# Fused two-matrix product with tanh: six plain row tiles in place of eight, the first weight slices by a second queue, a new order of all engines, and the last products' finish shared otherwise

## The chip, the cores and the metric

One core of a Trainium2 chip. The time is the device time of one execution in microseconds (us), the median of several. A span is the same execution as the hardware profiler sees it; on this kernel it is 1.7 to 2.2 us shorter than the device time. Engines are called TensorE (PE in the profile, its weight loads PEld), VectorE (DVE), ScalarE (ACT), GpSimd (POOL) and SyncE (SP, which here only issues transfers).

## The reference

```python
x: (16, 512, 1024) f32, w1, w2: (1024, 768) f32
y1 = np.matmul(x, w1)
y2 = np.matmul(x, w2)
return (np.tanh(y1) * y2).astype(np.float32)
```

There are 8192 rows, that is 64 row tiles of 128.

## The kernel before

The first `HEAD` row tiles are multiplied the plain way in bf16, while the weights are still arriving. All others go in pairs through a recursive scheme (Strassen's): seven products of half size (p1 to p7) in place of eight, in f16, on sums and differences of blocks of x (s1 to s4) and of w (t1 to t4). A "unit" is one pair with one of the two weights. Each half-size product is 4 matmuls of 384 columns, so a pair costs 2 x 7 x 4 = 56.

```python
HEAD = 8
WARM = 14                                         # matmuls on constants at the very start
PAIRS = (MT - HEAD) // 2
LOADS = ("x0 a0 x1 a1 x2 a2 x3 a3 a4 a5 a6 a7 b0 b1 b2 b3 b4 b5 b6 b7").split()   # x tiles; slices of w1 (a), w2 (b)
FILL = {"m00G0": 16, "m10G0": 4, "m20F0": 4}      # matmuls on constants, ahead of these
ORDER = {"pe": """T00 T01 m00G0 m00F0 T10 T11 ...""", "act": """...""", "dve": """...""", "dma": """..."""}   # [cut]
```

`ORDER` fixes each engine's queue for the head and the first ten units. In its names Tij is a transpose of an x tile on TensorE, mijFk and mijGk are plain matmuls of 512 and 256 columns (tile i, weight j, slice k), Lp, ax, rx, cx and Tx are a later x tile's load, sum of absolute values, scale, cast and transpose by DMA, and b11a ... t4b are weight blocks. From unit 10 on, times in slots of 0.65 us set the order. I call the seam between the two "the join".

```python
def load_w(t, k):
    pin(nc.sync.dma_start(w_f[t][:, k, :], wr[t][:, k, :]))

def product(i, t, n, bank, start, stop, cols=slice(0, Q)):
    a, b = PRODUCTS[n]
    for k in range(KH):                                     # four matmuls
        pin(nc.tensor.matmul(bank[:, cols], st[i, a][:, k, :], wt[t][b][:, k, cols], ...))

# a unit, cut to what the text needs
"p1":   pe               "seed": act, copies p1's bank, needs p1
"p6":   pe, needs seed   "c12", "c22": dve, sums of banks
"p4":   pe, needs c22    "f..": the outputs (tanh on act, multiply on dve)

# the last two units: GpSimd takes over two multiplies
if u == UNITS - 1:
    for h, c, due in ((0, "c12", 4.1), (1, "c22", 4.8)):
        ops[f"f{h}1"] = ("pool", 0.85, due, [c], final_pool, (u, c, h))
        ops[f"store{h}1"] = ("dma", 0.5, due + 0.1, [f"f{h}1"], store, (i, h, high, nc.scalar))

# later pairs
at(slot(z - 25), scale_x, i)
for h in range(2):
    at(slot(z - 24 + 4 * h), cast_x, i, h, "dve")
    at(slot(z - 24 + 4 * h), transpose_x, i, h)
```

## Time and profile before

| | before |
|---|---|
| time, median of the first 3 runs | 319.98 us (319.44 to 320.25) |
| profiled execution | 320.89 us, span 319.0 |
| first transposes of x0, of x1 on TensorE | 4.22 us, 8.13 us |
| first recursive product | 51.22 us |
| stop at the join | 101.60 to 102.34 and 103.64 to 104.26: 1.36 us |
| start of the last product to the end of the span | 5.12 us |

The chain of waits follows the run back from its last instruction, so it shows what sets the time; a list of waits shows only what an engine waited for; the timeline of TensorE shows also what it did in place of waiting. The prediction shows these lines.

### The profile page before, as it was taken

Reading aid. Unit: us, or ns where it says so; the run is one execution under the profiler, and the core shown is the slowest. Engines: PE = TensorE matmul, PEld = TensorE weight load, DVE = VectorE, ACT = ScalarE, POOL = GpSimd, SP = SyncE. Lnnn points to the kernel's source line nnn. Section 1 sums busy time; section 2 is a strip of 40 time slices with the busy share of each in tenths; the row PEclk is TensorE's granted clock in tenths of the full one; section 3 lists DMA queues with packets and bytes.
Section 4 is the critical chain, followed back from the end, with each engine's and each line's share of the span. In section 5 each row is a group of like instructions: output and inputs, shape, how many; then the busy total and the mean of one; then the engine's idle time right before and its main releaser. Section 6 shows DMA issues by size and latency. Waiting matters only on the chain.

```text
span 319.0 us, 5509 instructions
## 1 busy us (share of the span) xinstructions
PE 310.9 (97%) x1924; PEld 188.1 (59%) x1930; DVE 241.1 (76%) x559; ACT 227.6 (71%) x442; POOL 5.1 (2%) x10
## 2 busy tenths in 40 slices
PE   8999999999999999999999999999999999999994
PEld 5665665666555565555556565555555655555652
DVE  2557899686887897777778877777798777778742
ACT  1767896787767677787777778787777787776551
POOL 0000000000000000000000000000000000000004
PEclk9999999999999999999999999999999999999999
DMA  7999189969989999899999898998998999986222
GB/s 246 408 400 408 54 229 285 255 205 214 343 247 269 281 294 283 243 278 275 251 241 257 262 235 275 283 265 248 255 249 262 230 286 274 247 234 166 99 101 100
DMA packets 80187, 80.05 MB, mean 251 GB/s; under 512 B 61472, under 2 KB 61984, under 8 KB 80160
## 3 DMA queue, kind: packets, MB, share of 16 engines
q1 hardware_dynamic: 79872, 79.31, 87.7%
q8 instruction: 15, 0.25, 0.3%
q10 hardware_dynamic: 288, 0.39, 0.3%
q14 instruction: 12, 0.10, 0.1%
HBM read 39.85 MB, written 25.17 MB: 204 GB/s over the span
## 4 chain that ended last, share of the span: by engine, by line
PE 89%; DMA 8%; ACT 1%; DVE 1%; issue 0%; SPq 0%
PE bank L405 80%; DMA wf<-in_w_dram 6%; PE bank L271 5%; PE bank L274 3%; DMA x_f<-in_x_dram 2%; PE bank L243 1%; ACT junk L344 0%; DVE wb L258 0%; DVE o L441 0%; ACT th L435 0%; SPq L254 0%; SPq L217 0%; ACT bank L418 0%; DVE wp0r L354 0%; DVE w_inv L352 0%
## 5 line engine op out<-in xcount | busy, mean ns | idle before, releaser
L405 PE MATMUL bank<-t,s 128*128 128x384 f16 x672 | 127.6, 326 | 0.6 <-ACT u L422 0.6
L405 PEld LDWEIGHTS <-s 128*128 128x128 f16 x896 | 87.5, 98 | 59.4 <-issue 1.5
L405 PEld LDWEIGHTS <-xT 128*128 128x128 f16 x672 | 65.6, 98 | 45.3 <-issue 1.1
L405 PE MATMUL bank<-b,xT 128*128 128x384 f16 x448 | 90.6, 326 | 0.5 <-ACT bank L418 0.5
L427 DVE TENSOR_TENSOR c<-bank,u 128x384 f32<-128x384 f32 x56 | 31.0, 554 | 46.1 <-PE bank L405 45.6
L344 ACT ACTIVATE junk<-x_f 128x1024 bf16<-128x1024 f32 x56 | 58.7, 1049 | 1.7 <-DMA x_f<-in_x_dram 1.6
L435 ACT ACTIVATE th<-c,out_r 128x384 f32<-128x384 f32 x56 | 33.9, 609 | 23.2 <-DVE c L427 23.2
L405 PE MATMUL bank<-b,s 128*128 128x384 f16 x224 | 45.4, 326 | 0.0
L405 PE MATMUL bank<-t,xT 128*128 128x384 f16 x224 | 45.3, 325 | 0.0
L422 ACT ACTIVATE u<-bank 128x384 f32<-128x384 f32 x56 | 27.3, 488 | 20.1 <-PE bank L405 19.5
L364 DVE TENSOR_SCALAR x_h<-x_f,pr 128x1024 f16<-128x1024 f32 x54 | 40.1, 747 | 0.1
L435 ACT ACTIVATE th<-bank,out_r 128x384 f32<-128x384 f32 x56 | 32.2, 575 | 6.0 <-PE bank L405 6.0
L441 DVE SCALAR_TENSOR_TENSOR o<-bank,out_r,th 128x384 f32<-128x384 f32 x56 | 34.2, 611 | 2.9 <-PE bank L405 2.8
L418 ACT ACTIVATE bank<-bank 128x384 f32<-128x384 f32 x56 | 27.0, 483 | 9.9 <-DVE o L441 8.7
L427 DVE TENSOR_TENSOR c<-bank,s 128x384 f32<-128x384 f32 x56 | 31.0, 554 | 3.8 <-ACT th L435 1.3
L422 ACT ACTIVATE s<-bank 128x384 f32<-128x384 f32 x56 | 26.9, 483 | 8.3 <-PE bank L405 6.0
L441 DVE SCALAR_TENSOR_TENSOR o<-c,out_r,th 128x384 f32<-128x384 f32 x54 | 32.5, 607 | 0.1
L271 PE MATMUL bank<-wb,xTb 128*128 128x512 bf16 x122 | 31.2, 379 | 0.5 <-DVE wb L258 0.2
L386 DVE TENSOR_TENSOR s<-xT 128x512 f16<-128x512 f16 x56 | 23.0, 416 | 0.0
L274 PE MATMUL bank<-wb,xTb 128*128 128x256 bf16 x128 | 19.2, 272 | 0.6 <-DVE wb L258 0.5
L271 PEld LDWEIGHTS <-xTb 128*128 128x128 bf16 x128 | 12.3, 98 | 11.6 <-issue 0.8
L274 PEld LDWEIGHTS <-xTb 128*128 128x128 bf16 x128 | 12.5, 99 | 5.1 <-issue 0.7
(51 smaller groups left out, 156.2 us busy)
## 6 DMA issues: line engine op xcount, KB each, us to landing
x_f<-in_x_dram SPq DMA_DIRECT2D x64, 512.0 KB, 6.2
out_dram<-o SPq DMA_DIRECT2D x62, 384.0 KB, 3.4
wf<-in_w_dram SPq DMA_DIRECT2D x16, 384.0 KB, 9.4
xT<-x_h SPq DMA_TRANSPOSE x56, 3.7
out_dram<-o ACTq DMA_DIRECT2D x2, 192.0 KB, 2.0
out_dram<-o SPq DMA_DIRECT2D x2, 192.0 KB, 2.4
```

The costliest lines, as they stand in the source:

```text
L243: pin(nc.tensor.transpose(b[:, k * P:(k + 1) * P], hb[mt][:, k * P:(k + 1) * P], ident_b))
L271: pin(nc.tensor.matmul(bank, hx[mt][:, k, :], w_b[t][k][:, :F], start=k == 0, stop=k == KO - 1))
L274: pin(nc.tensor.matmul(bank[:, at_:at_ + G], hx[mt][:, k, :], w_b[t][k][:, F:], start=k == 0 and mt % 2 == 0, stop=k == KO - 1, skip_group ...
L344: pin(nc.scalar.activation(junk[:, :K], xs[HEAD + 2 * i + h], ACT.Abs, scale=2.0 ** -12, accum_out=pair_sum[i][:, h:h + 1]))
L364: pin(nc.vector.tensor_scalar(xh, xs.pop(mt), pair_r[i][:, h:h + 1], None, ALU.mult))
L386: pin((nc.vector if eng == "dve" else nc.gpsimd).tensor_tensor(s, st[i, a], st[i, b], op))
L405: pin(nc.tensor.matmul(bank[:, cols], st[i, a][:, k, :], wt[t][b][:, k, cols], start=start and k == 0, stop=stop and k == KH - 1, skip_gro ...
L418: pin(nc.scalar.activation(ub[u]["b"][:, :Q], ub[u]["a"][:, :Q], ACT.Copy))
L422: pin(nc.scalar.activation(c, ub[u][bank][:, :Q], ACT.Copy))
L427: pin(nc.vector.tensor_tensor(c, ub[u][bank][:, :Q], ub[u][other], ALU.add))
L435: pin(nc.scalar.activation(th, v, ACT.Tanh, scale=rs[i][:, 0, h:h + 1]))
L441: pin(nc.vector.scalar_tensor_tensor(o[:, h, q * Q + cols.start:q * Q + cols.stop], v, rs[i][:, 1, h:h + 1], tanhs[i, h, q][:, cols], ALU. ...
```

## The change

The intent is to take work out of TensorE, which sets the time: two more tiles go through the recursive products. This leaves fewer plain matmuls to cover the time in which the weights' blocks are made, so the loads are started earlier (four slices of w1 by ScalarE's queue) and the order of all engines is made anew. At the end, half of GpSimd's second multiply goes to VectorE.

```diff
-    HEAD = 8
-    WARM = 14
+    HEAD = 6
+    WARM = 18
+    EARLY = ("La0", "La1", "La2", "La3")
-    FILL = {"m00G0": 16, "m10G0": 4, "m20F0": 4}
+    FILL = {"m00F0": 3, "m00F1": 6}
     ORDER = { ... all four lists new [cut] ... }
-                    at(start, fn, *args)
+                    at(0.0 if name in EARLY else start, fn, *args)
     def load_w(t, k):
-        pin(nc.sync.dma_start(w_f[t][:, k, :], wr[t][:, k, :]))
+        eng = nc.scalar if f"L{'ab'[t]}{k}" in EARLY else nc.sync
+        pin(eng.dma_start(w_f[t][:, k, :], wr[t][:, k, :]))
+        pool_cols = slice(0, Q), slice(Q // 2, Q)
-            for h, c, due in ((0, "c12", 4.1), (1, "c22", 4.8)):
-                ops[f"f{h}1"] = ("pool", 0.85, due, [c], final_pool, (u, c, h))
+            ops["f01"] = ("pool", 0.85, 4.1, ["c12"], final_pool, (u, "c12", 0, pool_cols[0]))
+            ops["f11b"] = ("pool", 0.5, 4.8, ["c22"], final_pool, (u, "c22", 1, pool_cols[1]))
+            ops["f11"] = ("dve", 0.4, 4.8, ["c22"], final, (u, "c22", 1, 1, slice(0, Q // 2)))
-        at(slot(z - 25), scale_x, i)
+        late = 1.1 * (i == FIRST + 1)
+        at(slot(z - 25 + late), scale_x, i)
         for h in range(2):
-            at(slot(z - 24 + 4 * h), cast_x, i, h, "dve")
-            at(slot(z - 24 + 4 * h), transpose_x, i, h)
+            at(slot(z - 24 + late + 4 * h), cast_x, i, h, "dve")
+            at(slot(z - 24 + late + 4 * h), transpose_x, i, h)
```

Cut: `ELSEWHERE`, which moves single operations to another engine, the planned durations of the first loads, and the stores that go with the new finish.

More of the change, by code (lines that the diff above doesn't have):

```diff
@@ L55 @@
                "t3": ("dve", 50), "t4": ("dve", 52)})
+    EARLY = ("La0", "La1", "La2", "La3")
     ELSEWHERE = {
-        "e01": "dve", "e11": "dve", "e31": "dve", "ca1": "act", "hx6": "act", "e71": "act", "cx30":
-        "act", "cx31": "act"
+        "e01": "dve", "e11": "dve", "e20": "act", "e21": "dve", "e31": "dve", "ca0": "act", "ca1": "act",
+        "cb4": "act", "b22a": "dve", "cx11": "act", "cx31": "act", "cx61": "act"
     }
-    FILL = {"m00G0": 16, "m10G0": 4, "m20F0": 4}
+    FILL = {"m00F0": 3, "m00F1": 6}
@@ L62 @@
     ORDER = {
         "pe": """
-            T00 T01 m00G0 m00F0 T10 T11 m10G0 m10F0 m00F1 m00G1 m10F1 T20 T21 m20F0 m20F1 m20G0 m20G1 m00G2
-            m10F2 m00F2 m20F2 T30 T31 m00G3 m10F3 m20F3 m00F3 m30F0 m30F1 m30F2 m30F3 m30G0 m30G1 m30G2 m20F4
-            m00G4 m10F4 m00F4 m00G5 m00F5 m10F5 m20F5 m30G3 m20G2 m20G3 m20G4 m10G1 m20G5 m10F6 m20G6 m00F6
-            m20F6 m10G2 m10G3 m10G4 m10G5 m10G6 m30G4 m30G5 m30G6 m00F7 m20F7 m20G7 m30G7 m10G7 m10F7 m30F4
-            m30F5 m30F6 m30F7 m21G0 m01F0 m11F0 m31G0 m11F1 m21G1 m31G1 m01F1 m01F2 m11F2 m31G2 m31G3 m01F3
@@ L69 @@
-            m31G4 m01F4 m11F3 suma m00G6 m00G7 m21G2 m21G3 m21G4 m11F4 m21F0 m21F1 m21F2 m21F3 m21F4 m21F5
-            m31G5 m01F5 m01F6 m11F5 m11F6 m31G6 m01F7 m11F7 m31G7 T4 m31F0 m31F1 m31F2 m31F3 m31F4 m31F5 m31F6
-            m31F7 m01G0 m11G0 m11G1 m11G2 m11G3 m01G1 m01G2 m01G3 m11G4 m11G5 m11G6 m01G4 m01G5 m11G7 m40F0
-            m40F1 m40F2 T5 m40F3 m40F4 m40F5 m40F6 m40F7 m01G6 m50F0 m01G7 m50F1 m50F2 m50F3 m50F4 m50F5 m50F6
-            m50F7 sumb m21G5 m21G6 m21G7 T6 m21F6 m21F7 m41F0 m41F1 m41F2 m41F3 m41F4 m41F5 m41F6 m41F7 T7
@@ L74 @@
-            m40G0 m50G0 m50G1 m40G1 m50G2 m50G3 m50G4 m50G5 m50G6 m40G2 m40G3 m40G4 m50G7 m40G5 m40G6 m40G7
-            m51F0 m51F1 m51F2 m51F3 m51F4 m51F5 m51F6 m51F7 m41G0 m41G1 m41G2 m41G3 m41G4 m41G5 m41G6 m41G7
-            m51G0 m51G1 m51G2 m51G3 m51G4 m51G5 m51G6 m51G7 m70F0 m70F1 m70F2 m70F3 m70F4 m70F5 m70F6 m70F7
-            m60F0 m60F1 m60F2 m60F3 m60F4 m60F5 m60F6 m60F7 m61F0 m61F1 m61F2 m61F3 m61F4 m61F5 m61F6 m61F7
-            p1.0 m60G0 m70G0 m60G1 m60G2 m60G3 m60G4 m70G1 p5.0 m70G2 m70G3 m70G4 m70G5 m70G6 m70G7 m60G5
@@ L79 @@
-            m60G6 m60G7 p2.0 p1.1 m71F0 m71F1 m71F2 m71F3 m71F4 m71F5 m71F6 m71F7 p6.0 p5.1 m61G0 m61G1 m61G2
-            m71G0 m71G1 m71G2 m71G3 m71G4 m71G5 p7.0 p2.1 m71G6 m61G3 m61G4 m61G5 m61G6 m61G7 p3.0 p4.0 p6.1
-            p1.2 p3.1 p7.1 m71G7 p5.2 p2.2 p4.1 p6.2 p1.3 p3.2 p7.2 p5.3 p2.3 p4.2 p6.3 p1.4 p3.3 p7.3 p5.4
-            p2.4 p6.4 p4.3 p1.5 p3.4 p7.4 p5.5 p2.5 p4.4 p6.5 p1.6 p3.5 p5.6 p7.5 p6.6 p2.6 p4.5 p1.7 p3.6
-            p6.7 p2.7 p5.7 p7.6 p7.7 p3.7 p4.6 p4.7 p1.8 p1.9 p5.8 p5.9 p3.8 p3.9 p6.8 p2.8 p7.8 p2.9 p1.10
@@ L84 @@
-            p4.8 p6.9 p7.9 p5.10 p2.10 p4.9
+            T00 T01 m00F0 m00G0 T10 T11 m00F1 m00G1 m10F0 T20 m10G0 m10G1 m10F1 T21 m20G0 m20F0 m20F1 m20G1
+            m10G2 m20G2 m00F2 m00G2 m20F2 m10F2 T30 T31 m10G3 m00G3 m20F3 m10F3 m20G3 m00F3 m10F4 m10G4 m20F4
+            m20G4 m00G4 m00F4 m30G0 m30G1 m30G2 m30G3 m20G5 m10G5 m10F5 m20F5 m20G6 m10G6 m10F6 m30G4 m30G5
+            m30G6 m20G7 m10G7 m30G7 m10F7 m00F5 m00F6 m00F7 suma m11F0 m20F6 m20F7 m01F0 m00G5 m00G6 m00G7
+            m11F1 m01F1 m30F0 m30F1 m30F2 m30F3 m30F4 m30F5 m30F6 m30F7 m21F0 m21F1 m11F2 m21F2 m01F2 m11F3
@@ new lines @@
+            m21F3 m01F3 m31F0 m31F1 m31F2 m31F3 m21G0 m21G1 m21G2 m21G3 m31G0 m31G1 m31G2 m31G3 m01F4 m31G4
+            m21G4 m11F4 m01G0 m01G1 m11G0 m11G1 m01G2 m01G3 m01G4 m31F4 T4 m11F5 m11F6 m01F5 m31F5 m01G5 m01G6
+            m31F6 m01F6 m31G5 m31G6 m01F7 m31F7 m11F7 m31G7 T5 m40F0 m40F1 m40F2 m40F3 m40F4 m40F5 m40F6 m01G7
+            m40F7 m21G5 m21G6 m50F0 m50F1 m50F2 m50F3 m50F4 m50F5 m50F6 m50F7 m21F4 m21F5 m21G7 m21F6 m21F7
+            m11G2 m11G3 m11G4 m11G5 m11G6 m11G7 m40G0 m50G0 m50G1 m50G2 m50G3 m50G4 m50G5 m50G6 m50G7 m40G1
@@ new lines @@
+            m40G2 m40G3 m40G4 m40G5 m40G6 m40G7 sumb m41F0 m41F1 m41F2 m41F3 m41F4 m41F5 m41F6 m41F7 m41G0
+            m41G1 m41G2 m41G3 m41G4 m41G5 m41G6 m51G0 m51G1 m51G2 m51G3 m51G4 m51G5 m51G6 m51G7 m41G7 m51F0
+            m51F1 m51F2 m51F3 m51F4 m51F5 m51F6 m51F7 p1.0 p1.1 p5.0 p6.0 p2.0 p3.0 p7.0 p5.1 p6.1 p4.0 p2.1
+            p7.1 p1.2 p3.1 p4.1 p1.3 p6.2 p2.2 p5.2 p6.3 p2.3 p5.3 p7.2 p7.3 p3.2 p4.2 p3.3 p4.3 p1.4 p1.5
+            p5.4 p5.5 p2.4 p6.4 p6.5 p2.5 p7.4 p7.5 p3.4 p3.5 p4.4 p4.5 p1.6 p1.7 p5.6 p6.6 p2.6 p6.7 p2.7
@@ L85 @@
+            p7.6 p3.6 p5.7 p7.7 p4.6 p3.7 p1.8 p4.7 p1.9 p2.8 p6.8 p5.8 p5.9 p7.8 p1.10 p3.8 p4.8 p3.9 p6.9
+            p2.9 p2.10 p7.9 p5.10 p4.9
         """,
         "act": """
-            ca1 absa1 absa0 e21 absa2 absa3 absa4 absa5 absa6 absa7 tanh2F tanh2G tanh1F absb2 absb4 tanh0G
-            absb7 tanh3F tanh0F absb0 absb6 b21a b22a hx6 tanh5F tanh4F ax00 ax01 e71 b11b tanh4G b22b ax11
-            b21b tanh7F tanh6F ax10 ax20 seed.0 ax30 tanh6G f00.0 ax21 u2.0 seed.1 ax31 s5.0 s5.1 f11.0 f01.0
@@ L90 @@
-            u2.1 f10.0 seed.2 ax41 s5.2 f00.2 u2.2 seed.3 cx30 f01.2 f11.2 s5.3 f10.2 u2.3 seed.4 cx31 s5.4
-            f00.4 u2.4 ax40 seed.5 f01.4 f11.4 s5.5 ax50 f10.4 u2.5 seed.6 s5.6 ax51 f00.6 seed.7 u2.6 u2.7
-            s5.7 ax61 ax60 f10.6 f11.6 f01.6 s5.8 s5.9 seed.8 u2.8 seed.9 f00.8 f11.8 f10.8 u2.9 f01.8 seed.10
-            s5.10 f00.10
+            ca0 absa0 ca1 absa1 e20 absa2 absa3 absa4 absa5 absa6 absa7 tanh2G absb0 tanh1F tanh0G tanh2F cb4
+            tanh0F absb2 absb6 tanh3F absb4 ax00 absb7 ax01 b21a tanh4F tanh5F ax10 ax11 tanh4G ax20 cx11 b11b
@@ L94 @@
+            b22b seed.0 seed.1 s5.0 u2.0 ax21 b21b u2.1 f00.0 s5.1 f10.0 ax31 seed.2 ax30 seed.3 f11.0 u2.2
+            u2.3 s5.2 s5.3 f00.2 f01.0 ax40 cx31 f10.2 seed.4 ax41 seed.5 s5.4 s5.5 u2.4 u2.5 f11.2 f00.4 ax51
+            f01.2 ax50 f10.4 seed.6 f11.4 seed.7 f01.4 u2.6 s5.6 ax61 u2.7 s5.7 f00.6 f11.6 f10.6 seed.8 ax60
+            f00.8 u2.8 f01.6 s5.8 cx61 s5.9 seed.9 f10.8 seed.10 u2.9 f01.8 f11.8 f00.10 s5.10
         """,
         "dve": """
-            e00 e01 ca0 e10 e11 e20 ca2 ca3 e30 ca4 ca5 ca6 e31 ca7 parta cb0 cb1 cb2 cb3 cb4 cb6 scalea cb5
@@ L97 @@
-            hx4 cb7 b11a t1a mul0F e41 hx5 mul1F e51 mul3F mul0G partb scaleb mul2G e61 hx7 mul2F mul4F rx0
-            sx0 cx00 cx01 t1b mul5F t2a mul4G t2b t4b t3b s3.0 s1.0 rx1 cx10 sx1 cx11 mul6F s2.0 s4.0 t3a t4a
-            mul7F rx2 sx2 cx20 cx21 c22.0 c12.0 s1.1 s2.1 s3.1 s4.1 c12.1 c22.1 mul6G f00.1 f11.1 f10.1 rx3
-            sx3 c12.2 c22.2 s3.2 s1.2 s2.2 f00.3 s4.2 f01.1 c12.3 f01.3 c22.3 f11.3 f10.3 c12.4 c22.4 s1.3
-            s3.3 s2.3 f00.5 rx4 cx40 sx4 cx41 c12.5 c22.5 f01.5 s4.3 f10.5 f11.5 rx5 cx50 sx5 f00.7 c12.6
@@ L102 @@
-            c22.6 c22.7 s1.4 s2.4 cx51 s4.4 s3.4 c12.7 rx6 cx60 f10.7 f11.7 f01.7 s1.5 s3.5 c22.8 cx61 c12.8
-            s2.5 s4.5 c12.9 f00.9 c22.9 f01.9 f10.9 f11.9
+            e00 e01 e10 e11 ca2 e21 ca3 ca4 e30 ca5 ca6 e31 ca7 parta cb0 cb1 scalea b11a cb2 cb3 t1a b22a hx4
+            cb6 cb5 t2a e41 cb7 hx5 mul0F mul3F mul1F e51 t3a rx0 cx00 cx01 mul2G mul2F mul0G partb t4a rx1
+            cx10 scaleb mul4F sx0 mul4G s1.0 s2.0 s4.0 s3.0 sx1 t1b t2b t3b c22.0 rx2 sx2 cx20 t4b s1.1 c22.1
@@ L104 @@
+            f00.1 s2.1 c12.0 f10.1 s3.1 cx21 c12.1 s4.1 f11.1 rx3 cx30 c22.2 c22.3 s3.2 s1.2 f00.3 f01.1 c12.2
+            c12.3 s2.2 f10.3 mul5F rx4 cx40 s4.2 cx41 s3.3 c22.4 f11.3 c22.5 f00.5 s1.3 c12.4 f01.3 s2.3 f10.5
+            rx5 f11.5 s4.3 cx50 c12.5 f01.5 c22.6 sx3 cx51 c22.7 f00.7 s1.4 s2.4 sx4 s3.4 c12.6 c12.7 rx6 cx60
+            s4.4 sx5 f01.7 c22.8 f10.7 f11.7 s1.5 s2.5 c12.8 s3.5 c12.9 f00.9 c22.9 s4.5 f11.9 f01.9 f10.9
         """,
         "dma": """
-            Lx0 La0 Lx1 La1 Lx2 La2 Lx3 La3 La4 La5 La6 La7 Lb0 Lb1 Lb2 Lb3 Lb4 Lb5 Lb6 Lx4 Lb7 Lx5 Lx6 Lx7
@@ L107 @@
-            Lp00 Lp01 Lp10 st2 Lp11 Tx00 Lp20 Tx01 Lp21 st4 Lp30 Lp31 Tx10 Lp40 Tx11 Lp41 Tx20 Lp50 Tx21 st7
-            st6 store1.1 Tx30 st3 store0.1 Tx31 Lp51 st5 st1 st0 Lp60 Tx40 Lp61 Tx41 store0.5 store1.5 Tx50
-            Lp70 Tx51 Lp71 Tx60 store0.7 store1.7 Tx61 store0.3 store0.9 store1.9 store1.3
+            Lx0 La0 Lx1 La1 Lx2 La2 Lx3 La3 La4 La5 La6 La7 Lb0 Lb1 Lb2 Lb3 Lb4 Lx4 Lb5 Lb6 Lx5 Lb7 Lp00 Lp01
+            Lp10 Lp11 Tx00 Lp20 Tx01 st3 Lp21 Tx10 Lp30 st4 Tx11 Lp31 st1 Tx20 Lp40 Lp41 Tx21 st2 Lp50 Tx30
@@ L110 @@
+            Lp51 Tx31 Lp60 st5 Tx40 Lp61 st0 Tx41 Lp70 store1.5 Tx50 store0.5 Lp71 Tx51 store0.1 store1.1 Tx60
+            store0.7 store1.7 Tx61 store1.3 store0.3 store0.9 store1.9
         """,
@@ L442, in final, with scale_tanh, final_pool @@
                                                tanhs[i, h, q][:, cols], ALU.mult, ALU.mult))
-    def scale_tanh(i, h):
-        pin(nc.gpsimd.tensor_scalar(tanhs[i, h, 1], tanhs[i, h, 1], rs[i][:, 1, h:h + 1], None, ALU.mult))
-    def final_pool(u, src, h):
+    def scale_tanh(i, h, cols):
+        v = tanhs[i, h, 1][:, cols]
+        pin(nc.gpsimd.tensor_scalar(v, v, rs[i][:, 1, h:h + 1], None, ALU.mult))
+    def final_pool(u, src, h, cols):
         i = SEQUENCE[u][0]
@@ L450, in final_pool @@
             outs[i] = opool[0].tile([P, 2, N], f32, tag="o", name="o")
-        pin(nc.gpsimd.tensor_tensor(outs[i][:, h, Q:], ub[u][src], tanhs[i, h, 1], ALU.mult))
+        pin(nc.gpsimd.tensor_tensor(outs[i][:, h, Q + cols.start:Q + cols.stop], ub[u][src][:, cols],
+                                    tanhs[i, h, 1][:, cols], ALU.mult))
     def store(i, h, cols=slice(0, N), eng=nc.sync):
@@ L497, in unit_ops @@
             ops["store1"] = ("dma", 1.1, 9.5, ["f10", "f11"], store, (i, 1))
+        pool_cols = slice(0, Q), slice(Q // 2, Q)
         if u == UNITS - 2:
             for h in range(2):
-                ops[f"g{h}"] = ("pool", 1.0, 8 + h, [f"f{h}1"], scale_tanh, (i, h))
+                ops[f"g{h}"] = ("pool", 1.0, 8 + h, [f"f{h}1"], scale_tanh, (i, h, pool_cols[h]))
         if u == UNITS - 1:
@@ L507, in unit_ops @@
             ops["f00"] = ops["f00"][:2] + (5.8,) + ops["f00"][3:]
-            for h, c, due in ((0, "c12", 4.1), (1, "c22", 4.8)):
-                ops[f"f{h}1"] = ("pool", 0.85, due, [c], final_pool, (u, c, h))
-                ops[f"store{h}1"] = ("dma", 0.5, due + 0.1, [f"f{h}1"], store, (i, h, high, nc.scalar))
+            ops["f01"] = ("pool", 0.85, 4.1, ["c12"], final_pool, (u, "c12", 0, pool_cols[0]))
+            ops["f11b"] = ("pool", 0.5, 4.8, ["c22"], final_pool, (u, "c22", 1, pool_cols[1]))
+            ops["f11"] = ("dve", 0.4, 4.8, ["c22"], final, (u, "c22", 1, 1, slice(0, Q // 2)))
+            ops["store01"] = ("dma", 0.5, 4.2, ["f01"], store, (i, 0, high, nc.scalar))
+            ops["store11"] = ("dma", 0.5, 4.9, ["f11", "f11b"], store, (i, 1, high, nc.scalar))
             ops["store0"] = ("dma", 0.5, 6.5, ["f00"], store, (i, 0, low))
@@ L525, in op2 @@
         op(name, engine, COST[kind, engine], due, needs, fn, *args, engine)
+    STEP = {"x0": 2.2, "a0": 0.3, "x1": 1.75, "a1": 0.8, "x2": 1.4, "a2": 0.8, "x3": 1.6, "a3": 0.2}
     for n, what in enumerate(LOADS):
@@ L529 @@
         if what[0] == "x":
-            op(f"L{what}", "dma", 1.8 if i == 1 else 1.4, n - 200, [], load_head_x, i)
+            op(f"L{what}", "dma", STEP[what], n - 200, [], load_head_x, i)
         else:
-            op(f"L{what}", "dma", 1.01, n - 200, [], load_w, "ab".index(what[0]), i)
+            op(f"L{what}", "dma", STEP.get(what, 1.01), n - 200, [], load_w, "ab".index(what[0]), i)
     for mt in range(4):
```

## The prediction

> **What bounds the kernel now.** I read the page's busy times first, to find the fullest engine, then the chain of work that ended last, to see whether that engine sets the end. From the page, busy time and share of the span, and after it the chain in order of time (start, us, what), cut to the places that matter:
>
> ```profile
> PE 310.9 (97%) x1924; PEld 188.1 (59%) x1930; DVE 241.1 (76%) x559; ACT 227.6 (71%) x442; POOL 5.1 (2%) x10
> ```
>
> ```profile
> 65.70 36.08 PE bank L405 x220
> 101.78 0.02 issue
> 101.80 0.03 ACT u L422
> 101.83 0.36 issue
> 102.19 0.61 ACT th L435
> ...
> 104.26 210.44 PE bank L405 x1284
> 314.71 0.03 issue
> 314.73 0.62 DVE o L441
> ```
>
> TensorE is the bound: from 65.7 to 314.7 us the chain is products (L405) with one break, 101.78 to 104.26. The 1284 matmuls at the end take 210.44 us, 0.164 each. So a change pays what it takes out of TensorE's queue, plus the waits in it that it removes, less those that it makes. The list of TensorE's waits is short (under 4 us), but it hides filler: matmuls on constant data (L158) that fill waits for the loads. TensorE's timeline shows them (start, us, engine, line, what):
>
> ```profile
> 4.22 1.23 PE L228 MATMUL bank<-ident,x_f 128*128 128x128 f32 x8
> 5.29 1.91 PE L158 MATMUL bank<-ones 128*128 128x256 bf16 x16
> 7.04 0.27 PE L274 MATMUL bank<-wb,xTb 128*128 128x256 bf16 x1
> 7.15 0.38 PE L271 MATMUL bank<-wb,xTb 128*128 128x512 bf16 x1
> 8.13 1.09 PE L228 MATMUL bank<-ident,x_f 128*128 128x128 f32 x8 [0.60 <-DMA x_f<-in_x_dram]
> 9.06 0.60 PE L158 MATMUL bank<-ones 128*128 128x256 bf16 x4
> ```
>
> Useful work begins at 4.22 us, when the first row tile is there; x1 comes only at 8.13. Stretches tell how full the vector engines are (window; length; PE, PEld, DVE, ACT, POOL busy; clock; DMA share; GB/s):
>
> ```profile
> 27.50:51.00 23.50, 23.36 (x158) 14.31 (x160) 20.98 (x35) 20.29 (x27) 0.00 (x0) 1.00 0.67 210
> 104.00:200.00 96.00, 95.74 (x586) 57.21 (x586) 78.18 (x191) 70.77 (x145) 0.00 (x0) 1.00 0.97 264
> ```
>
> Between the plain tiles and the steady products VectorE (20.98 of 23.5) and ScalarE (20.29) are nearly full as well. That matters below.
>
> **What the Trainium skill says.** (1) "TensorE: Matmul & The Clock Gate", Back-to-back issue gap, gives the isolated gap as N/2.4 + 2.5 ns: 162.5, 215.8 and 109.2 ns for 384, 512 and 256 columns. The trace agrees: in the timeline four 384-column matmuls start every 0.65 us, 16 of 256 columns take 1.75, 24 of 512 take 5.18. The page also says that sustained streams are closer than that at 512 columns (131 ns); this trace has 216, and that decides. (2) "Perfetto Trace Analysis", Identifying the Most-Contended Engine, warns that matmul busy time is no measure of headroom; hence I rest on the chain and on start-to-start times, not on the 97%. (3) "DMA: Bandwidth & Descriptors", Issuing engines are not separate DMA queues: loads issued by two engines run on the same 16 DMA engines, and only issue time is saved. No run here has two load streams at once yet. In this trace the first eight loads' issues, 0.40 to 0.57 us each, run from 0.72 to some 4.5 us.
>
> **The change part by part.**
>
> *Two row tiles go from plain to recursive products.* A plain tile is 16 matmuls of 512 and 16 of 256 columns: 16 x (0.2158 + 0.1092) = 5.20 us; two, 10.40 us off. Tiles 6 and 7 also were transposed on TensorE, 0.45 us each (the chain's "x8" pieces of L243): 0.90 off. The pair becomes 2 halves x 7 products x 4 = 56 matmuls of 384: at 0.1625 it adds 9.10, at the steady 0.1639 9.18. Sum: -10.40 - 0.90 + 9.15 = **-2.15 us** on the path, the firmest term.
>
> *First w1 slices on ScalarE's queue.* Four x tiles go out on SyncE at once, four w1 slices on ScalarE (its issue list has them ahead of the table load, which now ends about 1.4 us later, before the first cast needs it). After x0 and a0, x1 and a1 no longer wait for issue. In the stretches of 1 us DMA moved 283, 401, 307, 254, 254, 394 GB/s from 2 to 8 us and about 400 afterwards, so there is roughly 0.5 to 1.2 us of early transfer to win. Against it, x0 now shares the engines with w1 slices: I allow up to 0.7 us later for the first transpose, and the four further warming matmuls (0.11 each) say that its author expects that too.
>
> *The filler and the waits in the head.* From 4.22 to 14.23 us TensorE did 4 transposed tiles (1.07 + 0.93 + 0.87 + 0.92 = 3.8 us, start to start), 8 matmuls of 512 (1.73) and 6 of 256 (0.66): 6.2 useful in 10.0, so 3.8 lost, 2.6 of it 24 fillers. After: 9 fillers (1.0), and I guess 1.2 us of idle as before: 2.2 lost. Less an estimated 0.4 for the later start: **-1.0 us** (0 to -1.8).
>
> *The new order at the join.* The stop near 102 us costs 0.74 + 0.62 = 1.36 us against the 0.65 rhythm (100.95 + 0.65 to 102.34; 102.34 + 1.30 to 104.26). The diff postpones pair 7's scaling by 1.1 slots there, that is, it was retuned. I give **-0.5** (0 to -1.4).
>
> *The last products.* 4.3 us follow the last matmul. GpSimd's last two multiplies take 1.96 us and end about 0.5 us after it; half of the second goes to VectorE. But the last VectorE multiply starts 0.02 us after the last product, and its store ends the run. **-0.1**.
>
> **The rivals.** *A: the vector engines can't have the first products ready, and TensorE stalls where it now never does.* Plain work is 6 x 5.20 = 31.2, transposes 3.8 + 0.9. From 4.6 us with 2.2 lost TensorE is through with it at about 42.7; the kernel before had its first L405 at 51.2 and mixed plain matmuls in until 65.5, the new order has hardly any left to mix in. ScalarE by then must have done (trace durations less the overlap of neighbours) 9 tanh x 0.5 = 4.5, five w2 sums 7.1, one cast 0.75, five x sums 6.0, one x cast 1.05, three w blocks 4.5: about 24 us since the first tanh at near 20 us, so the first seed copy is at 44 at best, and with the 3 us of waits that it had in 27.5 to 51, at 46. TensorE wants it at 42.7 + 3 x 0.65 = 44.6. VectorE from the first w2 cast (19 us) to the last of the first pair's four blocks: 15.7 to the pair's casts and 7.6 more, 42.3 at best, wanted by 44 to 46. So both are on the edge: I put **+1.2 us**, 0 to 3.5. For A: this count. Against: before, the same kind of plan ran with 0.7 us of stalls between 14 and 100 us.
> *B: the head gains nothing.* Round-robin holds x0 and x1 back; TensorE idles where fillers ran, and +1.0 takes the place of -1.0: about 319.2. For: 408 GB/s in the second slice, no room there. Against: 254 GB/s at 5 to 7 us.
> *C: all works and the join closes*: -2.15 - 1.8 - 1.36 - 0.1 = -5.4, 314.6. This is still inside 2%.
>
> **How the range and the chances follow.** 319.98 - 2.15 - 1.0 - 0.5 - 0.1 + 1.2 = 317.4. The range takes most of C at one end and A's or B's bad case at the other: 315.0 to 319.8. Two per cent is 6.4 us: faster than 313.6 is out of reach of every sum above, slower than 326.4 needs a stall of 9 us, over twice my worst. Chances: 0.03 faster, 0.96 same, 0.01 slower.
>
> **What would show each step right or wrong.** Products: 1624 L405 matmuls, 96 each of L271's and L274's kin and 16 bf16 transposes, at the same spacing of 162.5 ns. Head: x1's transposes before 8.1 us, the last of x3's before 14.2, and fewer than 3 us lost between. Rival A: TensorE waits on ScalarE (b blocks, seed) or VectorE (s or t blocks) between 42 and 52 us; over 2 us of them would push it above 318.6. Join: no stop of a microsecond near 100 us. Tail: 4.2 to 4.3 us after the last matmul. The prediction is wrong if a stall of several microseconds appears in the transition, if the x transposes of the first pairs land late because loads and stores crowd them, or if the first tile comes over a microsecond later than 4.2.

## The result, and the profile after

The changed kernel took **317.2 us** (median of 4 runs, 317.08 to 317.27). The kernel before took 319.84 in 4 runs (319.44 to 320.25). The ratio is 0.9917, with a 95% interval of 0.99 to 0.9934; a ratio is the mean time of one kernel's runs over that of the other's of the same rounds, so it is not quite the ratio of the medians. Executions over 1.5% slower than the fastest of the same kernel are left out of the means. In a later job the changed kernel took 317.15 and the kernel before 319.46 (0.9931, 0.9914 to 0.9948).

The busy times and the chain of waits of the changed kernel (its products are on line 401 now):

```profile
PE 307.9 (98%) x1890; PEld 185.5 (59%) x1895; DVE 244.8 (78%) x571; ACT 230.5 (73%) x453; POOL 4.3 (1%) x10
```

```profile
42.74 1.48 ACT b L313
44.21 0.02 issue
44.24 1.83 DVE t L318
46.07 0.03 issue
46.09 37.70 PE bank L401 x231
83.79 3.09 DMA xT<-x_h
86.88 1.09 ACT junk L340 x2
87.97 6.29 DMA xT<-x_h
...
96.70 212.80 PE bank L401 x1300
```

The last, long piece has the spacing of before: 212.80 / 1300 = 0.164 us. But the chain no longer runs along TensorE from 46 to 96 us. It leaves it at 83.79 for a tile transposed by DMA, which took 6.29 us to land, and comes back at 96.70. And it comes to the first products by way of a weight block on ScalarE (b, L313) and one on VectorE (t, L318). So there are two new places where vector work and transfers hold TensorE up.

TensorE's timeline in the head shows that the filler has nearly gone, that x0's transposes start 0.90 us later than before (5.12 for 4.22) and x1's 0.59 earlier (7.54 for 8.13):

```profile
5.12 1.37 PE L223 MATMUL bank<-ident,x_f 128*128 128x128 f32 x8
6.33 0.49 PE L153 MATMUL bank<-ones 128*128 128x256 bf16 x3
6.84 0.39 PE L267 MATMUL bank<-wb,xTb 128*128 128x512 bf16 x1
7.07 0.27 PE L270 MATMUL bank<-wb,xTb 128*128 128x256 bf16 x1
7.54 1.09 PE L223 MATMUL bank<-ident,x_f 128*128 128x128 f32 x8 [0.20 <-DMA x_f<-in_x_dram]
8.47 0.82 PE L153 MATMUL bank<-ones 128*128 128x256 bf16 x6
```

The stretch from there to the first recursive product (window; length; PE, PEld, DVE, ACT and POOL busy; clock; DMA share; GB/s) has TensorE full and the vector engines at 85 and 81%:

```profile
13.63:43.19 29.56, 29.35 (x192) 18.20 (x194) 25.21 (x51) 24.04 (x41) 0.00 (x0) 1.00 0.86 301
```

Then come the first products, on TensorE's timeline:

```profile
43.19 0.81 PE L401 MATMUL bank<-b,xT 128*128 128x384 f16 x4
44.25 0.81 PE L401 MATMUL bank<-b,xT 128*128 128x384 f16 x4 [0.25 <-ACT b L313]
44.90 0.81 PE L401 MATMUL bank<-t,s 128*128 128x384 f16 x4
46.09 0.81 PE L401 MATMUL bank<-t,s 128*128 128x384 f16 x4 [0.38 <-DVE t L318]
```

In the rhythm of 0.65 us the second group would start at 43.84 and the fourth at 45.55, so the stalls are 0.41 + 0.54 = 0.95 us. At the join the same reckoning gives one stop, 95.69 to 96.70, 1.01 us:

```profile
95.04 0.81 PE L401 MATMUL bank<-b,xT 128*128 128x384 f16 x4
96.70 0.81 PE L401 MATMUL bank<-t,xT 128*128 128x384 f16 x4 [0.84 <-DVE c L423]
```

### The profile page after: what moved, and what is told of

Its sections match the earlier page's. It is cut to its first block, busy times and chain, and to the rows that moved or that the text cites. A ratio compares the mean times of both kernels' runs of the same rounds, so it can differ in the third digit from the quotient of the medians.

```text
span 315.3 us, 5481 instructions
## 1 busy us (share of the span) xinstructions
PE 307.9 (98%) x1890; PEld 185.5 (59%) x1895; DVE 244.8 (78%) x571; ACT 230.5 (73%) x453; POOL 4.3 (1%) x10
## 4 chain that ended last, share of the span: by engine, by line
PE 86%; DMA 6%; DVE 3%; ACT 2%; issue 1%; DVEq 0%; SPq 0%; ACTq 0%
PE bank L401 79%; PE bank L267 4%; DMA x_f<-in_x_dram 3%; DMA xT<-x_h 3%; PE bank L270 2%; PE bank L223 1%; ACT junk L340 1%; DVE x_h L360 1%; DVE o L287 1%; DVE t L318 1%; ACT b L313 0%; DVE c L423 0%; DVE o L437 0%; ACT x_h L362 0%; DVE t L322 0%
## 5 line engine op out<-in xcount | busy, mean ns | idle before, releaser
L401 PE MATMUL bank<-t,s 128*128 128x384 f16 x696 | 131.6, 326 | 0.4 <-DVE t L318 0.4
L401 PEld LDWEIGHTS <-s 128*128 128x128 f16 x928 | 90.6, 98 | 61.1 <-issue 0.8
L401 PEld LDWEIGHTS <-xT 128*128 128x128 f16 x696 | 67.9, 98 | 48.0 <-issue 2.2
L401 PE MATMUL bank<-b,xT 128*128 128x384 f16 x464 | 93.8, 326 | 0.2 <-ACT b L313 0.2
L340 ACT ACTIVATE junk<-x_f 128x1024 bf16<-128x1024 f32 x58 | 60.8, 1049 | 2.6 <-DMA x_f<-in_x_dram 2.5
L414 ACT ACTIVATE bank<-bank 128x384 f32<-128x384 f32 x58 | 27.8, 481 | 12.7 <-DVE o L437 10.1
L437 DVE SCALAR_TENSOR_TENSOR o<-c,out_r,th 128x384 f32<-128x384 f32 (+1 forms) x57 | 34.3, 606 | 0.4 <-ACT th L431 0.2
L267 PE MATMUL bank<-wb,xTb 128*128 128x512 bf16 x91 | 23.9, 380 | 0.2
L270 PE MATMUL bank<-wb,xTb 128*128 128x256 bf16 x96 | 14.6, 273 | 0.0
L260 ACT ACTIVATE junk<-wf 128x768 bf16<-128x768 f32 (+1 forms) x13 | 12.8, 988 | 1.4 <-DMA wf<-in_w_dram 1.2
L267 PEld LDWEIGHTS <-xTb 128*128 128x128 bf16 x96 | 9.3, 99 | 7.5 <-DVE xTb L231 0.3
```

The source lines that it names most:

```text
L260: pin(nc.scalar.activation(junk[:, :n * N].rearrange("p (k n) -> p k n", n=N), w_f[t][:, k:k + n, :], ACT.Abs, accum_out=asum_w[t][:, j:j ...
L267: pin(nc.tensor.matmul(bank, hx[mt][:, k, :], w_b[t][k][:, :F], start=k == 0, stop=k == KO - 1))
L270: pin(nc.tensor.matmul(bank[:, at_:at_ + G], hx[mt][:, k, :], w_b[t][k][:, F:], start=k == 0 and mt % 2 == 0, stop=k == KO - 1, skip_group ...
L340: pin(nc.scalar.activation(junk[:, :K], xs[HEAD + 2 * i + h], ACT.Abs, scale=2.0 ** -12, accum_out=pair_sum[i][:, h:h + 1]))
L414: pin(nc.scalar.activation(ub[u]["b"][:, :Q], ub[u]["a"][:, :Q], ACT.Copy))
L437: pin(nc.vector.scalar_tensor_tensor(o[:, h, q * Q + cols.start:q * Q + cols.stop], v, rs[i][:, 1, h:h + 1], tanhs[i, h, q][:, cols], ALU. ...
```

## The experiments

The kernels of one job ran on one chip and shared the runs of the kernel before; medians of different jobs are therefore compared only through their ratios to it. Even that is rough: the kernel with the weight blocks first, below, had a ratio of 0.9923 in one job and 0.9899 in another, which is 0.8 us apart. Differences of this size are safe only within one job. All outputs are right.

### The kernel before, profiled again

No edit.

> The kernel before itself, for a second profile. Its first profile came from an execution of 320.89 us with a span of 319.0, while the other executions have spans of 317.2 to 318.2. Theory: a typical execution has the same head (first transposes at 4.2, x3's near 13.3), first L405 near 51.2, and a stop at the join that is longer or shorter; the 1 us between the first profile and the median lies in the join or in waits of the head, not in the spacing of the products. Rival: the spacing of matmuls itself differs (0.164 and 0.163), which would be 2 us over 1568.

Measured: 319.52 us (318.94 to 320.79); ratio to the kernel before in the same rounds 0.9995, as it should be. The profiled execution was the fast one this time: 318.94 us, span 317.2. TensorE's timeline and, below it, the chain:

```profile
4.24 1.07 PE L228 MATMUL bank<-ident,x_f 128*128 128x128 f32 x8
...
7.32 1.09 PE L228 MATMUL bank<-ident,x_f 128*128 128x128 f32 x8
```

```profile
49.59 0.65 PE bank L405 x4
...
102.47 210.44 PE bank L405 x1284
```

x1 was there at 7.32, where the first profile had 8.13, and the first recursive product started at 49.43 (TensorE's timeline) instead of 51.22. From there to the end of the span it is 317.2 - 49.43 = 267.77 us here and 319.0 - 51.22 = 267.78 us in the first profile. So **all of the difference between the two profiles lies before the first recursive product**, in when the first loads land; what follows it is the same to 0.01 us. The next two kernels, which change only the head, agree: 267.87 and 267.68 us follow their first products. Of what I expected, the join and the rival (the spacing) are refuted. The waits of the head remain, but I had put the first product of a typical execution near 51.2. The median time in this job is 0.58 us above that of the profiled execution; if that lies in the head as well, a typical execution has its first product near 50.0 us. The first profile, which the prediction read, was 1.2 us slower than that.

### The kernel before without filler

```diff
-    FILL = {"m00G0": 16, "m10G0": 4, "m20F0": 4}
+    FILL = {}
```

> The kernel before without its 24 filler matmuls (the 14 at the start stay). Theory (fillers lie in waits for loads and cost nothing; the 3.8 us lost in the head are waits for data): same time within 0.3 us, x1's transposes still near 8.1 us, clock 0.99 or more in the head. Rival 1 (they run ahead of ready work and cost their 2.6 us partly): 0.5 us or more faster. Rival 2 (without them TensorE's granted clock falls): slower, with a clock clearly under 1 in the first 15 us.

Measured: 319.94 us (318.97 to 320.67), ratio 1.0004 (0.9985 to 1.0022), same as the kernel before. Where 16 fillers were, TensorE's timeline now has a plain wait:

```profile
6.88 0.27 PE L274 MATMUL bank<-wb,xTb 128*128 128x256 bf16 x1 [1.41 <-DVE wb L258]
```

The first plain matmul starts at 6.88, as with filler (6.88 in the second profile of before). The filler costs nothing and gains nothing that this test can see; it lies in time that the loads leave. The granted clock read 1.00 in each microsecond from 3 to 12 us, and the spacing of the matmuls, which in the last experiment shows what this column does not, is the usual one (three of 256 columns from 11.70 to 12.03). So rival 2 is refuted too.

### The second queue alone, in the kernel before

```diff
+    EARLY = ("La0", "La1", "La2", "La3")
...
-                    at(start, fn, *args)
+                    at(0.0 if name in EARLY else start, fn, *args)
...
-        pin(nc.sync.dma_start(w_f[t][:, k, :], wr[t][:, k, :]))
+        eng = nc.scalar if f"L{'ab'[t]}{k}" in EARLY else nc.sync
+        pin(eng.dma_start(w_f[t][:, k, :], wr[t][:, k, :]))
```

> The kernel before (eight plain tiles, its own order) with one part of the change alone: the first four w1 slices on ScalarE's queue. Theory (the loads come 0.6 us earlier from x1 on, but the first tile 0.9 later, and the old order with its 24 fillers uses little of it): x1's transposes near 7.5 in place of 8.13, a gain of 0 to 0.6 us against the kernel before. Rival 1 (the second queue carries the head's gain whatever the order): 0.8 us or more faster. Rival 2 (later first tile, all else held by fillers): 0.3 to 0.9 us slower.

Measured: 321.18 us (319.50 to 322.12), ratio 1.0033 (1.0008 to 1.0059): by the means 1.1 us **slower** than the kernel before, by the medians 1.4. The first product starts at 51.72. TensorE's timeline says why:

```profile
5.09 1.94 PE L230 MATMUL bank<-ident,x_f 128*128 128x128 f32 x8 [0.89 <-DMA x_f<-in_x_dram]
6.83 2.89 PE L160 MATMUL bank<-ones 128*128 128x256 bf16 x16
```

x0 lands at 5.09 instead of 4.24, because four w1 slices now share the DMA engines with it. The 14 warming matmuls end before that, TensorE idles for 0.89 us, and the 16 fillers after the transposes start 0.171 us apart, where the kernel before has 0.109 us: the array ran at less than full speed, and the old order puts those fillers ahead of ready work. x1's transposes follow only at 9.88. The loads as such were no slower (383 to 418 GB/s in every microsecond from 3 to 11 us). So my theory's gain of 0 to 0.6 us was wrong, and rival 2 was the direction. The change brings the second queue together with 18 warming matmuls and few fillers; which of these the second queue needs was not tested one by one.

### One queue in the changed kernel

```diff
-    EARLY = ("La0", "La1", "La2", "La3")
+    EARLY = ()
```

> The changed kernel with all first loads on SyncE's queue again, in the old alternation x0 a0 x1 a1; nothing else moves (TensorE's order is the same). Theory (the second queue gives the head's gain): x1's transposes start near 8.1 us in place of 7.54, x3's near 13.3 in place of 12.76, and TensorE gets 0.5 to 1.2 us less done by 14 us; the rest is delayed by as much: 317.2 + 0.8 = 318.0 us (317.6 to 318.5). Rival 1 (the gain is from the new matmul order and fewer fillers, and the queue is hidden): 317.2, within 0.3. Rival 2 (the ScalarE-held stalls at 43 to 46 us come anyway at fixed times, set by vector work, so a later head is absorbed there): 317.2 too, but with x1's transposes late and the stalls near 44 us shorter.

Measured: 318.23 us (317.31 to 319.17), ratio 0.9949 (0.9932 to 0.9966). x0's transposes start at 4.34, x1's at 8.15, x3's at 13.47, and the first product at 44.01, that is 0.82 us later than in the changed kernel. The first of the two stalls near 44 us is then gone, so that the fourth product group comes at 46.62, only 0.53 later than 46.09. The profiles thus agree with the theory as to when data comes, and with rival 2 in that part of the delay is absorbed where ScalarE holds TensorE up anyway. But it was not kept: the stop at the join was 1.31 us (96.21 to 97.52), and from the first product to the end it is 272.09 us, against 272.11 in the changed kernel. The time does not settle the size: the changed kernel itself ran in another job (0.9931, 0.9914 to 0.9948), and the two intervals overlap; the difference of the ratios, 0.0018, would be 0.6 us, and against the first measurement (0.9917) it would be 1.0.

### The old finish in the changed kernel

```diff
-        pool_cols = slice(0, Q), slice(Q // 2, Q)
+        pool_cols = slice(0, Q), slice(0, Q)
-            ops["f01"] = ("pool", ...   ops["f11b"] = ("pool", ...   ops["f11"] = ("dve", ...   [and their stores]
+            for h, c, due in ((0, "c12", 4.1), (1, "c22", 4.8)):
+                ops[f"f{h}1"] = ("pool", 0.85, due, [c], final_pool, (u, c, h, pool_cols[0]))
+                ops[f"store{h}1"] = ("dma", 0.5, due + 0.1, [f"f{h}1"], store, (i, h, high, nc.scalar))
```

> The changed kernel with the last products' finish as in the kernel before (GpSimd takes both whole halves, VectorE none). The prediction gave this part 0.1 us; the profiles show 5.12 us (before) and 5.17 us (after) from the start of the last product to the end, so the theory is: no difference, 317.2 within 0.3, the last VectorE multiply about 0.2 us earlier and GpSimd's last one about 0.4 us later. Rival (GpSimd's second multiply and its store set the end): 0.3 to 0.5 us slower.

Measured: 318.05 us (317.29 to 319.13), ratio 0.9945 (0.9925 to 0.9965). From the start of the last product to the end of the span it is 316.2 - 311.23 = 4.97 us, against 315.3 - 310.13 = 5.17 with the new finish and 5.12 before. So no gain of the new finish can be seen: VectorE's last multiply, which the end waits for, now stands behind an extra one (310.12 to 310.69 in the changed kernel). Nor is a loss shown: the same piece takes 5.08 to 5.17 us in the other profiles with the new finish, and 4.99 to 5.20 in those of the kernel before and its variants. That this run's median lies above that of the changed kernel in another job is no effect of the finish that the profile shows; the profile has something else in it, a stop at the join from 95.74 to 97.73, 1.99 us, with the same order of every engine up to there. The tile that it waits for landed 7.3 us after its transpose was issued, where the changed kernel's profile had 6.3. The stop at the join thus differs from execution to execution.

### The changed kernel again

No edit.

> The changed kernel itself again, as the yardstick of this chip and of how far it scatters. Theory: 317.2 to 317.6 us; the stop near 95.7 us moves between 1 and 2 us from run to run, because the transposed tile it waits for landed after 6.3 us in one profile and 7.3 in another, so that single runs scatter by up to 1 us. Rival (a fixed stop): scatter under 0.3 us.

Measured: 317.15 us (316.87 to 318.85, 6 runs). Five of the six lie within 0.42 us and one is 1.6 us above them; the profiled one had a stop at the join of 0.90 us. That such an outlier is a long stop is argued, not shown, as only one execution is profiled.

### The weight blocks first on ScalarE

In the changed kernel ScalarE waited, just before the blocks that the first products need, for the load of a tile that is needed much later. Its timeline:

```profile
40.55 1.06 ACT L340 ACTIVATE junk<-x_f 128x1024 bf16<-128x1024 f32 x1 [1.90 <-DMA x_f<-in_x_dram]
...
41.60 1.13 ACT L362 ACTIVATE x_h<-x_f,pr 128x1024 f16<-128x1024 f32 x1
42.64 3.03 ACT L313 ACTIVATE b<-wf,wp1r 128x1536 f16<-128x1536 f32 x2
45.58 0.84 ACT L414 ACTIVATE bank<-bank 128x384 f32<-128x384 f32 x2
```

The edit lets the cast, the two blocks (b11b, b22b) and then the sum (ax20) run in this order:

```diff
-  ... tanh4G ax20 cx11 b11b b22b seed.0 ...
+  ... tanh4G cx11 b11b b22b ax20 seed.0 ...
```

> The changed kernel with one edit in ScalarE's order: the two blocks of w2 (b11b, b22b) go ahead of the fifth x sum (ax20), for whose load ScalarE sat idle 1.90 us until 40.55. Theory (TensorE's two stalls at 43.84 to 44.25 and 45.55 to 46.09, 0.95 us in all, are this wait passed on): b11b ends near 41.3 us, the first seed copy runs near 44.2, TensorE starts its products without a stop of over 0.1 us, and the time falls by 0.6 to 0.95, to 316.4. Rival 1 (the chain ends at the transposed x tiles and the join near 95.7, which don't move, so that the gain is given back there): stalls gone at 44 us, stop at 95.7 grown to near 2 us, 317.1. Rival 2 (VectorE's t block holds the second stall, as the wait list has it): first stall gone, second stays, 316.9.

The first try's profile fell in a state with a TensorE clock of 0.657 and a span of 461.7 us, so nothing is read from it. Its five other runs took 316.88 to 317.94 us (ratio 0.9923, 0.9907 to 0.9938).

> The changed kernel with the two blocks of w2 (b11b, b22b) ahead of the fifth x sum (ax20) on ScalarE, once more, as the profile of the first try fell in a state with a TensorE clock of 0.657. Theory (ScalarE's 1.90 us of waiting for that load is what stalls TensorE at 43.8 and 45.6): first seed copy near 44.2, no stop over 0.1 us between 43 and 47, and 0.6 to 0.95 us faster than the changed kernel of the same rounds unless the join takes it back. Rival 1 (given back at the join): stop near 95 us longer by as much, difference under 0.3 us. Rival 2 (VectorE's t block holds the second stall): a stop of 0.4 to 0.55 us remains near 45.

Measured: **316.30 us** (316.21 to 316.62, 4 runs), ratio 0.9899 (0.9886 to 0.9912), against 317.15 and 0.9931 (0.9914 to 0.9948) for the changed kernel in the same rounds: 0.85 us by the medians, with intervals that do not overlap, and all four runs lie below all six of the changed kernel (316.87 to 318.85). The first try's ratio of 0.9923 had been no better than the changed kernel's in its own jobs (0.9917 and 0.9931); with no changed kernel beside it, it neither supports nor refutes the gain. TensorE's, VectorE's and ScalarE's timelines:

```profile
43.07 1.46 PE L401 MATMUL bank<-b,xT 128*128 128x384 f16 x8
44.37 1.46 PE L401 MATMUL bank<-t,s 128*128 128x384 f16 x8
```

```profile
43.88 1.81 DVE L318 SCALAR_TENSOR_TENSOR t<-wf,wp1r,b 128x1536 f16<-128x1536 f32 x1
```

```profile
39.67 3.04 ACT L313 ACTIVATE b<-wf,wp1r 128x1536 f16<-128x1536 f32 x2
...
43.92 0.47 ACT L414 ACTIVATE bank<-bank 128x384 f32<-128x384 f32 x1 [0.17 <-PE bank L401]
```

Both stalls are gone. The t block on VectorE still ends only at 45.69, yet the fourth product group started at 45.02 in an unbroken run of eight matmuls. So it was not the t block that it waited for, though the list of waits of the changed kernel put 0.38 us down to it: there the t block (to 46.06) and ScalarE's copy of the bank (L414, the first to 46.05) ended at the same moment, and the list names the one that came last. It was the copy (the "seed", now done at 44.39), delayed by ScalarE's wait for a load. The profile of experiment (1) below, which has ScalarE's old order, agrees: its fourth group started at 46.23, ahead of the end of the t block (46.26), and its list names the copy. The join kept its stop (94.62 to 95.71, 1.09 us), so rival 1, that the gain is given back there, is refuted.

### Three tries at the join

The changed kernel's tile that lands late (the transpose issued at 87.97) had its input at 85.75, but stood in SyncE's queue behind two output stores and a load. Behind it VectorE has the second cast of the eighth pair (0.75 us) ahead of the sum c22 that TensorE waits for. The edits are

```diff
(1)  late = 1.1 * (i == FIRST + 1)          ->  2.1     # casts of the eighth pair later: c22 first
(2)  dma: Tx60 store0.7 store1.7 Tx61 ...   ->  Tx60 Tx61 store0.7 store1.7 ...
(3)  (1), (2) and the weight blocks first
(4)  (3), with four later stores (store1.3, store0.3, store0.9, store1.9) emitted 2.5 to 6 us later
```

(1):

> The changed kernel with the eighth pair's scaling and casts delayed by 2.1 slots in place of 1.1, so that VectorE does the sum c22 ahead of the second cast (0.75 us) at the join. Theory (the stop of 1.01 us at 95.69 is VectorE's order: c22 stood behind that cast): c22 ends some 0.7 us earlier, stop about 0.3 us, time 316.6 (316.4 to 316.9). Rival (the transposed tile that landed at 94.27 after 6.29 us sets it, and VectorE would be late anyway): stop stays at about 1 us, 317.2. Second rival: the later cast makes a later transpose late, and a new stop of as much appears after 96 us.

Measured: 317.61 us (316.47 to 318.20), ratio 0.9929 (0.9912 to 0.9946). From the start of the s block to the end of c22 VectorE took 1.70 us (94.99 to 96.69), where the changed kernel took 2.35 (94.29 to 96.64), so the order of VectorE is worth 0.65 us there. But in this execution the first tile was late (x0's transposes at 5.84, the first product at 43.64) and the transposed tile too (6.9 us after issue), and the stop was 0.92 us again. The time settles nothing.

(2):

> The changed kernel with one edit in SyncE's order: the transpose of pair 6's second tile goes ahead of two output stores (and so of the load behind them). In the changed kernel it was issued at 87.97 us, though its input was ready at 85.75, and landed at 94.27. Theory (the join's stop is that queue order): issued at about 86.0, landed by 91 to 92, VectorE's s block no longer waits, c22 ends by 96.1 in place of 96.64; stop 0.3 to 0.5 us in place of 1.0 to 2.0, time lower by 0.5 to 1.2 us, and scatter smaller. Rival (the DMA engines are just full there, and what goes ahead delays something else): the stores land later, output buffers come free later and a stop of like size appears after 96 us; no difference.

Measured: 316.81 us (316.41 to 318.36), ratio 0.9920 (0.9903 to 0.9936), against 0.9931 for the changed kernel in the same rounds: not to be told apart. The transpose was issued at 85.49 and landed in 4.8 us, VectorE no longer waited for its tile, but the stop was still 0.76 us: now VectorE's own order, the cast ahead of c22, set it. The transfer was one of two causes in a row, and to remove one shows the other.

(3):

> The candidate for a better kernel: w2's blocks first on ScalarE, pair 6's transpose ahead of the stores on SyncE, and the eighth pair's casts at 2.1 slots. Theory: stalls of 0.95 us near 44 gone, the stop near 95.7 under 0.3 us; 317.3 - 0.95 - 1.0 = 315.4 us (315.0 to 316.0). Rival (gains at 44 us only make TensorE arrive sooner at the join, where data, not order, sets the time): 316.3 or more, with a stop of 1 us or more left near 95.

Measured: 316.39 us (315.66 to 317.99), ratio 0.9903 (0.9882 to 0.9923), no better than the weight blocks alone (316.30 in the same rounds). The stop at 95 us shrank to 0.1 us, and a new one came one pair later. SyncE's timeline has the next pair's second transpose behind three stores and a load, and TensorE's has the stop:

```profile
96.34 1.83 SPq L368 DMA_TRANSPOSE xT<-x_h  x1
```

```profile
105.21 0.81 PE L401 MATMUL bank<-t,xT 128*128 128x384 f16 x4 [1.33 <-DVE c L423]
```

Its tile landed 7.1 us after issue, at 103.44; VectorE's sums follow, and TensorE stood from 103.71 to 105.21, 1.50 us. The time is the rival's, though the place is not: what was gained at the join was given back a pair later.

(4):

> The kernel of the three joined edits (w2 blocks first, pair 6's transpose ahead of stores, casts at 2.1 slots) with four output stores emitted 2.5 to 6 us later, so that pair 7's second transpose goes ahead of three of them. In the three joined edits that transpose was issued at 96.34 us, landed at 103.44 and TensorE stopped 1.50 us at 103.7. Theory (the stop wandered there because of the queue ahead of the transpose): it is issued by 95.5, lands by 101 and the stop is under 0.5 us: 315.4 (315.0 to 316.0), some 1 us under the three joined edits' median of 316.39. Rival (whatever goes ahead, the DMA engines are too full near the join, and the next late tile stops TensorE as long): 316.2 or more.

Measured: 316.24 us (315.16 to 317.35), ratio 0.9888 (0.9866 to 0.991). The order does what was expected of it: the transpose is issued at 97.24 in an execution that is nearly 2 us behind, and the chain shows TensorE without a stop from the first product on:

```profile
45.08 72.57 PE bank L402 x444
...
117.65 192.04 PE bank L402 x1172
```

444 matmuls in 72.57 us are 0.1634 each, the join included. From the first product to the end it is 270.49 us, the least of all: 271.23 with the weight blocks alone, 271.75 in (3), 272.11 in the changed kernel. Yet the median is where (3) and the weight blocks alone had it, and the runs scatter by 2.2 us; the expected 315.4 was only reached by two of the six (315.16 and 315.26). The profiled execution was the slowest of the six, and its loss is in the head:

```profile
7.46 0.84 PE L154 MATMUL bank<-ones 128*128 128x256 bf16 x3
8.10 0.63 PE L268 MATMUL bank<-wb,xTb 128*128 128x512 bf16 x1
```

The three fillers start 0.213 us apart, twice the usual 0.109. x0 had come at 5.72, 0.6 us later than in the changed kernel's profile, TensorE had idled 0.66 us just then, and x1's transposes ran at 8.73; the first product started at 44.91 in place of 43.0. With the stalls and the stop taken away, no wait is left downstream to absorb such a start. That this is what the other slow runs had is an inference; of this kernel one profile shows it.

This kernel and the weight blocks alone are the fastest that I ran: by the ratios 1.1 and 1.0% under the kernel before. The measurements don't tell the two apart.

## Why the prediction was right or wrong

The time, 317.2 for 317.4 predicted, was right, and so was its main term. Some of the other terms were mis-sized, and they cancelled, so that the agreement to 0.2 us is in part luck. For the sum I use typical executions: the kernel before with a span of 317.7 (the middle of its runs beside the second profile of it, 317.7 to 317.9, and of those beside the changed kernel, 317.6 to 317.7) and the changed kernel with 315.3, so -2.4 us. (In the other jobs the middle of before is 318.0 to 318.1; by the medians of two jobs the change brought 2.6 and 2.3.)

| term | predicted | measured |
|---|---|---|
| products and plain work | -2.15 | -2.15 by count and spacing: 1624 matmuls, 0.1625 us apart where unbroken |
| head | -1.0 | about -0.6 (up to -1.0 with a span of 318.1 for before) |
| stalls at the first products (rival A) | +1.2 | +0.95 |
| the join | -0.5 | 1.36 to 1.01: -0.35, and up to +0.6 in other runs |
| last products | -0.1 | 5.12 to 5.17: +0.05 |
| what is left: small gaps between products | none | about -0.3; the profiles show 0.1 of it ahead of the join and 0.1 after it (time less count times spacing: 0.31 to 0.20, and 1.62 to 1.53) |
| sum | -2.55 | -2.4 |

**The products** were as counted.

**The head** is the term whose baseline was wrong. The prediction took 3.8 us of lost time from one profile, that of an execution of 320.89 us, when the median was 319.98 and stood beside it. The second profile of before shows that the whole difference between its executions is the head. The useful work ahead of the first product is 6.1 us less in the changed kernel: 42.2 (36.4 plain, 5.6 transposes, 0.2 sums; the plain matmuls that before left for later are not in it) against 36.1 (31.2, 4.7, 0.2). A typical before has its first product at 317.7 - 267.8 = 49.9, so without any gain the changed kernel would have it at 43.8; it has it at 43.19: 0.6 gained, or up to 1.0 with the slower jobs' before. Against the first profile it would be 51.22 - 6.1 - 43.19 = 1.9, against the second 0.1. Within the head the prediction's signs hold, lost time of 2.2 us expected and 1.9 found (8.51 us from 5.12 to 13.63, with 6.66 of useful work), but the later start was 0.9 and not 0.4.

That ScalarE's queue would win 0.5 to 1.2 us of early transfer was right of the transfer: 390 to 411 GB/s from 3 to 7 us, where before had 401, 307, 254 and 254. "DMA: Bandwidth & Descriptors", Issuing engines are not separate DMA queues, says that only issue time is saved and that loads interleave on the same engines; the traces agree, with the first tile 0.9 us later. What the prediction did not see is that the second queue alone makes the old kernel about 1 us slower.

**Rival A** came as described, in place and size: TensorE reached the first products at 43.19 (42.7 predicted) and waited on ScalarE's b block and on its copy, which ran at 45.58 (44 to 46 predicted). The experiment with the blocks first shows the cause: not ScalarE's sum of work, which that count was about, but one wait of 1.90 us for a load. The count had 3 us of waits in it, as a lump from the kernel before, without knowing where they would be. One of its sums is off: stalls of over 2 us would, by its own terms, have put the time above 318.2 (317.4 - 1.2 + 2), not 318.6.

**The join** was predicted to have no stop of a microsecond; it has one of 1.0 us, in one run of 2.0. The prediction read from the diff that the join was retuned, which was right, and inferred that the stop closed, which was not: it has other causes now, a transposed tile that lands late and VectorE's order behind it. That a transposed tile would land late because loads and stores crowd it stands among the prediction's signs of being wrong; it came, and cost about 1 us. **The last products** show no gain, as the extra multiply went ahead of the one that ends the run; at the most 0.2 us are at stake.

What stays open: the size of the second queue's part within the changed kernel (0.6 to 1.0 us by ratios of different jobs, not secured), and whether the outliers of single runs are late first tiles or long stops at the join.

## What to carry to other kernels

Before you read a cost from a profile, compare the profiled execution's time with the median: here it was 0.9 us slower, all in one phase, and that phase's loss was overrated by over 1 us. When work is taken off the engine that sets the time, list what must be ready when it arrives, and in each engine's queue look for an instruction that waits for something needed later; here moving one such instruction gave 0.85 us in the job that measured both, a third of what the whole change had brought. A stop with two causes in a row shrinks only when both are removed, and then watch for it one step further on.

## What the Trainium skill lacked or had wrong

- "TensorE: Matmul & The Clock Gate", Back-to-back issue gap, gives about 131 ns as the sustained spacing of 512-column matmuls with their weight loads; here 24 of them took 5.18 us, 216 ns each, which is its own formula for the isolated gap, and 384 columns took 162.5 ns.
- The same section's cold formula, N/1.2 (213 ns for 256 columns), agrees with 0.213 us in the head of the last kernel; but the granted clock read 1.00 in those microseconds, so the profile's clock column did not show it. The page warns that clock events in traces are unreliable; here the spacing of matmuls on constants was the check.
- "DMA: Bandwidth & Descriptors", Issuing engines are not separate DMA queues, says what a second queue saves; no page says what it costs the transfer that is needed first: 0.85 us here (x0's transposes at 5.09 for 4.24 in the kernel before), and with the old order 1 us in all. In nine profiles with two queues these transposes start at 5.09 to 5.84, in four with one at 4.21 to 4.34.
- "DMA: Bandwidth & Descriptors", DMA Transpose (X-bar), gives constraints, and no page gives the time from issue to landing. Here a transpose of a 128 x 1024 f16 tile landed in 3.9 us in the median, and in 6.3 to 7.3 us where it stood behind two stores or three and a load.
